# One encoder kernel on one core: a third tap group on TensorE, its taps one step later, the bias table moved to POOL's and SP's queues, and a projection of two products per weight tile in place of three

## The chip, the cores and the metric

The kernel runs on one core of one Trainium2 chip. The time is that of one execution on the device, in microseconds (us). The kernel before took 2296.82 us, the median of three runs (2295.39 to 2298.47). PE is TensorE (PEld its weight loads), DVE is VectorE, ACT is ScalarE, POOL is GpSimd and SP is SyncE. SP computes nothing here; it issues DMAs. A name with a q behind it (ACTq, SPq) is that engine's queue of instructions, in which DMA issues stand.

## The reference

Input x is 256 tokens of 2048 channels, float32. There are two layers, each a mixer and a feed-forward part, with RMS norms in front and residual sums behind:

```python
for i in range(2):
    h = rmsnorm(x, mix_norm[i])
    m = conformer_conv(h, ...) if i == 0 else diff_attention(h, ...)
    x = x + m
    h = rmsnorm(x, ffn_norm[i])
    x = x + conv_ffn(h, ...)        # 2048 -> 2 x 5632, 3 causal taps, silu(gate) * val, -> 2048
return rmsnorm(x, final_norm_g)

def conformer_conv(h):              # the mixer of layer 0
    a, gate = split(h @ w_in + b_in)            # 2048 -> 2 x 2048
    u = causal_dwconv(a * sigmoid(gate), dw_w)  # 31 taps for each channel
    return silu(layernorm(u)) @ w_out + b_out

def diff_attention(h):              # the mixer of layer 1: 16 heads, two 64-wide maps each
    # scores + bias[head, bucket(k - q)], masked by chunks of 64,
    # softmax(first) - lambda * softmax(second), times v, rmsnorm, @ w_o
```

## The kernel before, in words

Activations lie transposed: channels on the 128 partitions, 256 tokens along the free axis. Every large product is made of float32 values split into a high and a low part (`hi`, `lo` for weights, index 0 and 1 of an activation tile for x), and is the sum hi*x_hi + hi*x_lo + lo*x_hi.

Weights come in steps of 512 KB (four 128-row blocks of 256 columns). For each step, SP loads `raw` (5 buffers, `load_w`), ACT copies it into `hi` (6 buffers), and DVE or POOL subtracts to get `lo` (6 buffers, `split_w`, lines 142 to 154). The loop `run` goes through the steps; before the products of step s it has the weights of step s+4 prepared. Four steps make one output tile pair (`pair`), accumulated in a PSUM tile `pp` (2 buffers). After the products of a step, work that was put down with `at(n, ...)` n steps earlier is issued, then six depthwise taps on DVE (`tap_step`), then, at the last step of a pair, its `post`.

In `pair` there are two ways to make the products of one weight block. With `merged` there are three products of 256 columns, all into the same 256 columns of PSUM (line 217). Without it, `hi` is multiplied by x_hi and x_lo side by side, 512 columns (lines 224 and 226), and `lo` by x_hi into the second 256 columns (lines 223 and 227); the two halves of PSUM are added afterwards. The projection w_in of layer 0's mixer is `merged`.

That projection has 16 tiles of four steps. `post` of tile i takes it out of PSUM times the norm's factor (line 436, DVE), makes the sigmoid (line 438, ACT), and writes u into `cpad[i % 3]` (line 440, DVE). Then the depthwise convolution of 31 taps starts. The first 4*G[i] taps are made on PE: u is stored to DRAM (`ud`, line 452), read back four times with shifts (`R`, line 456; both DMAs are issued by ACT), and multiplied by small diagonal matrices `dg`, which POOL makes (line 458). `taps` (line 470) does these products, `at(4)` after `post`. The remaining 31 - 4*G[i] taps are additions on DVE (line 513). The list G was 2 for tiles 0 to 10, then 3, 3, 5, 6, and 0 for the last tile, which goes another way (`last_taps`). Behind the last tile stand a layer norm and the product with w_out.

`attn_setup` (line 719) is called ahead of the first step of layer 0's feed-forward part. It loads a one-hot table and the relative bias, multiplies them, and stores the result 128 times into a DRAM table `d1` of 3 MB (line 732; in the trace the table is called d and its source Z). Much later, in the attention, `bias(h)` reads a skewed 128x256 block of it for each head (`bm`, line 809) and POOL sets one corner to the mask value (line 810). All of these DMAs are issued by ACT. The norm ahead of the feed-forward part gets its factor from a power on POOL (`rsqrt_cols`, line 286), and ACT copies it into `rstd` (line 348).

The order on each engine is made by a list scheduler that simulates the program; it moved the first two `bm` reads far ahead of the attention. Within `with tc.high_priority()` instructions are preferred.

Of the kernel before, what the change touches and what calls it, by code (L numbers as in the profile page):

```python
# [8 lines left out]
F32 = mybir.dt.float32  # L9
F32R = mybir.dt.float32r  # L10
AF = mybir.ActivationFunctionType
ALU = mybir.AluOpType
AX = mybir.AxisListType
ET = mybir.EngineType
P = 128
S = 256
# [5 lines left out]
MASK = -1.0e30  # L22
# [3 lines left out]
class Cfg:  # L26


    def __init__(self, d, f, kc=4):
        self.D, self.F = d, f  # L30
        self.KT = d // P
        self.FT = f // P
        self.H = d // (2 * HD)
        self.KC = kc
        self.NW = kc * 256
        self.kcs = [(i, kc) for i in range(0, self.KT, kc)]
        full = self.KT // 2
        first = self.FT % full or full
        self.chunks = [(0, first)] + [(i, full) for i in range(first, self.FT, full)]
        self.VK = kc // 2  # L40
        self.NA, self.NB = self.KT + self.KT // 2 + 1, 8

        self.G = [2] * (self.KT - 5) + [3, 3, 5, 6, 0]

        self.ND = 18

# [15 lines left out]
class Builder:  # L62
# [363 lines left out]
    def conv_module(self, nin, nout):  # L426
        c, a = self.c, self.a
        nc = self.nc
        KT = c.KT
# [2 lines left out]

        def post(i, ps):
            with self.tc.high_priority():
                t = self.b2("E")
                nc.vector.tensor_tensor(t, ps[:, :, 0:S], nin["rstd"].unsqueeze(1).to_broadcast([P, 2, S]), ALU.mult)
                sg = self.b1("G")
                nc.scalar.activation(sg, t[:, 1, :], AF.Sigmoid, bias=self.col("bin", KT + i))
                u = self.cpad[i % 3]
                nc.vector.scalar_tensor_tensor(u[:, CK - 1:CK - 1 + S], t[:, 0, :], self.col("bin", i), sg, ALU.add,  # L440
                                               ALU.mult)
                if i == KT - 1:
                    nc.scalar.activation(self.c2(), sg[:, 0:2], AF.Silu)
            gm = max(c.G)
            if i == KT - 1:
                self.at(0, lambda: last_taps(u, dgl))
                return

            g = c.G[i]
            n = 4 * (g - 1) + S  # L450
            ud = self.dr.tile([P, UW], F32, tag="ud", name=self.nm("ud"), bufs=2)
            nc.scalar.dma_start(ud, u)
            R = self.ph1.tile([P, 4, 4 * (gm - 1) + S], F32, tag="R", name=self.nm("R"), bufs=2)
            udv = ud.rearrange("(j c) n -> c j n", j=4)
            for s in range(4):
                nc.scalar.dma_start(R[s * 32:(s + 1) * 32, :, :n], udv[:, :, s:s + n])  # L456
            dg = self.ph1.tile([P, 4 * gm, 32], F32, tag="dg", name=self.nm("dg"))[:, :4 * g, :]
            nc.gpsimd.tensor_tensor(dg, self.cmask.unsqueeze(1).to_broadcast([P, 4 * g, 32]),
                                    self.col("wq", 4 * sum(c.G[:i]), 4 * g).unsqueeze(2).to_broadcast([P, 4 * g, 32]), ALU.mult)
            self.at(4, lambda: taps(i, u, R, dg))  # L460
            if i == 0:

                for j in range(0, c.ND, 4):
                    t = self.b2("Y" if j < 16 else "A").rearrange("p a (b s) -> p (a b) s", b=2)[:, :min(4, c.ND - j), :]
                    n = t.shape[1]
                    nc.gpsimd.tensor_tensor(t, self.ident.unsqueeze(1).to_broadcast([P, n, P]),
                                            self.col("cw", (KT - 1) * CK + j, n).unsqueeze(2).to_broadcast([P, n, P]), ALU.mult)
                    dgl.extend(t[:, x, :] for x in range(n))
# [174 lines left out]
        off = 0  # L643
        for i in range(KT):
            off = self.pair(a["w_in"], off, c.kcs, lambda k: nin["xh"][k], lambda ps, i=i: post(i, ps),
                            lo="v" if i == 0 else "vg" if i == 1 else "g", merged=True)
        off = 0
        for pr in range(KT // 2):
            def post2(ps, pr=pr):
                self.x_add(ps, pr, bias="bout")  # L650
                self.x_done(nout, pr)
                if pr == KT // 2 - 1:
# [3 lines left out]
                            lo="g" if pr < 2 else "v")  # L656
# [62 lines left out]
    def attn_setup(self):  # L719

        nc, c, a = self.nc, self.c, self.a
        H = c.H
        rb = self.ph2.tile([NB, H], F32, name="rb")
        nc.scalar.dma_start(rb, a["relb"])
        oh = self.b2("Z").rearrange("p a s -> p (a s)")[:NB, :384]
        nc.scalar.dma_start(oh, a["oneh"])
        ps = self.psx("o", [P, 384])
        nc.tensor.matmul(ps[:H, :], rb, oh, start=True, stop=True)
        tb = self.b2("Z").rearrange("p a s -> p (a s)")[:H, :384]
        nc.vector.tensor_copy(tb, ps[:H, :])  # L730
        d1 = self.dr.tile([H, P, 384], F32, name="d1")
        nc.scalar.dma_start(d1, tb.unsqueeze(1).to_broadcast([H, P, 384]))
        self.bflat = d1.rearrange("h p d -> (h p d)")
        lm = self.c2()
        nc.vector.tensor_tensor(lm[:HD], self.col("lam", 0, 2)[:HD], self.col("lam", 2, 2)[:HD], ALU.mult)
        ps = self.psx("o", [P, 2])
        nc.tensor.matmul(ps, self.ones[:HD, :], lm[:HD], start=True, stop=True)
        e = self.c2()
        nc.scalar.activation(e, ps, AF.Exp)
        self.nlam = self.const.tile([P, 1], F32, name="nlam")  # L740
        nc.vector.tensor_tensor(self.nlam, e[:, 1:2], e[:, 0:1], ALU.subtract)
        nc.vector.tensor_scalar(self.nlam, self.nlam, -LAMBDA_INIT, None, ALU.add)
        self.sg = self.const.tile([P, 1], F32, name="subg")
        nc.vector.tensor_scalar(self.sg, self.col("subg", 0), 1.0 - LAMBDA_INIT, None, ALU.mult)
        self.AT = []
        for i in range(2):
            self.AT.append((self.ph2.tile([P, 2, S], F32R, name=f"at{i}"), self.ph2.tile([P, P], F32, name=f"au{i}")))

    def attention(self, nin, nout):
        c, a = self.c, self.a  # L750
        nc = self.nc
        H, KT = c.H, c.KT
        V, U, O = {}, {}, {}

        def v_group(g, off):
            box = {}
# [47 lines left out]
            self.at(2, lambda: scores(h, q, k, qk))  # L804

        def bias(h):
            bm = self.ph2.tile([P, S], F32, tag="bm", name=self.nm("bm"), bufs=2)
            o = h * P * 384 + P - 1
            nc.scalar.dma_start(bm, self.bflat[o:o + P * 383].rearrange("(p d) -> p d", d=383)[:, :S])
            nc.gpsimd.memset(bm[0:64, S - 64:], MASK)  # L810
            return bm

        def scores(h, q, k, qk):
            bm = bias(h)
            ps = [self.psx("s", [P, 2, S]) for _ in range(2)]

            comp = [slice(cc * HD, (cc + 1) * HD) for cc in range(2)]
# [63 lines left out]
        off = voff = 0  # L881
        for h in range(H):
            if h % 4 == 0:
                voff = v_group(h // 4, voff)
            off = self.pair(a["w_qk"], off, c.kcs, lambda k: nin["xh"][k], lambda ps, h=h: qk_post(h, ps))
        off = 0
        held = []
        for pr in range(KT // 2):
# [146 lines left out]
```

## Time and profile before

| | |
|---|---|
| median of three runs | 2296.82 us |
| the profiled execution's own time | 2303.02 us |
| its span (first to last instruction) | 2300.4 us |
| PE busy | 2224.6 us, 97% |
| DVE, ACT, POOL busy | 73%, 52%, 12% |
| mean granted TensorE clock | 0.985 of full speed |
| DMA | 417.15 MB, 181 GB/s |

Busy time is the union of an engine's instructions. Where one engine fills the span, only its idle stretches and the time of its own instructions can shorten the run. The projection w_in with its taps lies between 6 and 262 us, the layer norm ends at 286 us, the product with w_out at about 381 us. The first feed-forward part begins there, and the attention lies in the stretch from about 1130 to 1490 us.

### The profile page before, as it was taken

The numbers are of one execution on the slowest core, as the hardware profiler recorded it, in microseconds if no ns is written. First come the engines' busy times: TensorE is split into PE (matmuls) and PEld (weight loads), VectorE is DVE, ScalarE is ACT, GpSimd is POOL, SyncE is SP. The second block draws the span as 40 slices with busy tenths as digits, with TensorE's granted clock in tenths as the row PEclk, the third lists the DMA queues.
The fourth block names the chain that finished last, engine by engine and source line by source line (L and its number), as shares of the span: only waits on it lengthen the run. The fifth ranks groups of instructions, "written<-read, shape, count | busy, mean of one in ns | idle before, by whom it ended". The sixth has DMA issues, their size and how long they took to land.

```text
span 2300.4 us, 34637 instructions
## 1 busy us (share of the span) xinstructions
PE 2224.6 (97%) x13294; PEld 1947.9 (85%) x13294; DVE 1670.9 (73%) x2539; ACT 1205.7 (52%) x1788; POOL 281.4 (12%) x189
## 2 busy tenths in 40 slices
PE   6899799799999999999999999999999999999998
PEld 6788688688888888888888888888888888888887
DVE  5788876577777767677766777677777777676774
ACT  5333265455555555455655555555555555554554
POOL 5678510000000000000111011010000000000002
PEclk9999899899999999999999999999999999999999
DMA  6766356766666666666655555466666666666663
GB/s 230 195 193 190 111 159 179 191 198 187 190 188 188 187 188 190 188 190 188 188 179 159 168 168 166 140 200 183 189 188 190 186 190 185 191 187 190 189 187 100
DMA packets 126885, 417.15 MB, mean 181 GB/s; under 512 B 14176, under 2 KB 28288, under 8 KB 126720
## 3 DMA queue, kind: packets, MB, share of 16 engines
q1 hardware_dynamic: 110736, 398.30, 56.8%
q10 hardware_dynamic: 15984, 16.65, 3.5%
q8 instruction: 104, 1.70, 0.3%
q14 instruction: 61, 0.50, 0.1%
HBM read 407.44 MB, written 7.45 MB: 180 GB/s over the span
## 4 chain that ended last, share of the span: by engine, by line
PE 88%; DMA 5%; DVE 4%; issue 1%; ACTq 0%; ACT 0%; POOL 0%; POOLq 0%; SPq 0%; DVEq 0%
PE pp L226 47%; PE pp L227 24%; PE pp L224 4%; PE pp L217 3%; PE pp L223 2%; DMA R<-ud 2%; DMA ud<-cpad 2%; DMA d<-Z 2%; PE pp L774 1%; PE pp L775 1%; PE pp L776 1%; DVE s L513 1%; DVE cpad L440 1%; PE s L475 0%; ACTq L456 0%
## 5 line engine op out<-in xcount | busy, mean ns | idle before, releaser
L226 PE MATMUL pp<-act,hi 128*128 128x512 f32 x3902 | 1382.9, 396 | 21.1 <-DVE E L256 13.0
L227 PE MATMUL pp<-act,lo 128*128 128x256 f32 x3902 | 1096.5, 281 | 0.0
L150 ACT CAST hi<-raw 128x1024 fp32r<-128x1024 f32 x752 | 787.6, 1049 | 536.0 <-PE pp L226 179.3
L152 DVE TENSOR_TENSOR lo<-raw,hi 128x1024 fp32r<-128x1024 f32 x686 | 844.3, 1231 | 283.0 <-ACT hi L150 281.2
L226 PEld LDWEIGHTS pp<-act,hi 128*128 128x128 f32 x3902 | 733.3, 188 | 182.9 <-DVE E L256 13.3
L227 PEld LDWEIGHTS pp<-act,lo 128*128 128x128 f32 x3902 | 739.1, 189 | 10.4
L226 PE MATMUL pp<-actb,hi 128*128 128x512 f32 x856 | 306.7, 396 | 0.0
L227 PE MATMUL pp<-actb,lo 128*128 128x256 f32 x856 | 240.4, 281 | 0.0
L321 POOL TENSOR_TENSOR ssq<-ssq,Z 128x512 f32<-128x512 f32 x24 | 35.6, 1481 | 1532.1 <-ACT Z L317 1532.0
L217 PE MATMUL pp<-act,hi 128*128 128x256 f32 x1088 | 209.3, 294 | 11.4 <-ACT act L267 6.0
L217 PEld LDWEIGHTS pp<-act,hi 128*128 128x128 f32 x1088 | 178.0, 200 | 19.3 <-DVE act L268 6.6
L226 PEld LDWEIGHTS pp<-actb,hi 128*128 128x128 f32 x856 | 160.6, 188 | 38.3 <-issue 0.6
L152 POOL TENSOR_TENSOR lo<-raw,hi 128x1024 fp32r<-128x1024 f32 x66 | 159.4, 2434 | 56.0 <-ACT hi L150 52.4
L256 DVE TENSOR_TENSOR E<-pp,E 128x512 f32<-128x512 f32 x104 | 71.8, 690 | 128.2 <-ACT E L254 127.9
L227 PEld LDWEIGHTS pp<-actb,lo 128*128 128x128 f32 x856 | 161.5, 189 | 0.2
L217 PE MATMUL pp<-act,lo 128*128 128x256 f32 x544 | 158.4, 291 | 2.8 <-DVE lo L152 2.8
L254 ACT COPY E<-pp 128x512 f32<-128x512 f32 x104 | 60.8, 585 | 186.9 <-PE pp L224 161.6
L370 ACT COPY E<-pp 128x512 f32<-128x512 f32 x109 | 63.9, 586 | 169.5 <-PE pp L224 161.8
L677 DVE SCALAR_TENSOR_TENSOR Y<-fpad,prm,Y 128x256 f32<-128x256 f32 x352 | 146.7, 477 | 0.0
L372 DVE TENSOR_TENSOR x<-pp,x 128x512 f32<-128x512 f32 x101 | 69.7, 690 | 89.4 <-ACT E L370 89.0
L674 ACT ACTIVATE Y<-fpad,prm 128x256 f32<-128x256 f32 x176 | 96.3, 596 | 48.2 <-DVE fpad L670 48.2
L513 DVE SCALAR_TENSOR_TENSOR s<-cpad,cprm,s 128x256 f32<-128x256 f32 x214 | 97.5, 482 | 24.8 <-PE s L475 22.6
(218 smaller groups left out, 1890.8 us busy)
## 6 DMA issues: line engine op xcount, KB each, us to landing
raw<-in_w_up_dram SPq DMA_DIRECT2D x352, 512.0 KB, 4.0
raw<-in_w_down_dram SPq DMA_DIRECT2D x176, 512.0 KB, 4.0
raw<-in_w_in_dram SPq DMA_DIRECT2D x64, 512.0 KB, 4.5
raw<-in_w_qk_dram SPq DMA_DIRECT2D x64, 512.0 KB, 3.6
raw<-in_w_out_dram SPq DMA_DIRECT2D x32, 512.0 KB, 4.1
raw<-in_w_v_dram SPq DMA_DIRECT2D x32, 512.0 KB, 3.7
raw<-in_w_o_dram SPq DMA_DIRECT2D x32, 512.0 KB, 3.7
R<-ud ACTq DMA_DIRECT2D x44, 130.0 KB, 5.1
```

Of the source, the lines that this page charges most:

```text
L150: nc.scalar.copy(hi[:, :n], raw[:, :n])
L152: eng.tensor_tensor(lo[:, :n], raw[:, :n], hi[:, :n].bitcast(F32), ALU.subtract)
L217: nc.tensor.matmul(ps[:, 0:S], w[:, kk, cs], xt[:, x, :], start=(k == first and n == 0), stop=(k == last and n == 2))
L224: nc.tensor.matmul(*main, start=False, stop=True)
L226: nc.tensor.matmul(*main, start=(k == first), stop=False)
L227: nc.tensor.matmul(*corr, start=False, stop=False)
L256: nc.vector.tensor_tensor(t, ps[:, :, 0:S], cs, ALU.add)
L370: nc.scalar.copy(cs, ps[:, :, S:])
L372: nc.vector.tensor_tensor(x, ps[:, :, 0:S], x, ALU.add)
L513: nc.vector.scalar_tensor_tensor(acc, u[:, j:j + S], self.col("cw", i * CK + j), acc, ALU.mult, ALU.add)
L674: nc.scalar.activation(y[:, j, :], u[:, j, FK - 1:], AF.Identity, scale=self.col("fw", ch * FK + FK - 1), bias=self.col("fb", ch))
L677: nc.vector.scalar_tensor_tensor(y[:, j, :], u[:, j, q:q + S], self.col("fw", ch * FK + q), y[:, j, :], ALU.mult, ALU.add)
```

## The change

- G is 3 for tiles 0 to 12: eleven tiles get one more group of taps on PE and four fewer on DVE.
- The projection w_in is made with one product of 512 and one of 256 columns per weight block, but for the last tile. `post` now copies the second half of PSUM out (ACT), adds it to the first half in PSUM, and multiplies there too; sigmoid and u read from PSUM.
- `taps` of tiles 0 to 13 are issued five steps after `post` in place of four.
- `attn_setup` issues its three DMAs from POOL in place of ACT, and writes the mask value into the table itself, with 16 further DMAs from POOL.
- `bias(h)` reads its block through SP, ahead of the first step of head h, in place of ACT and just ahead of the scores; the memset on POOL goes.

```diff
-        self.G = [2] * (self.KT - 5) + [3, 3, 5, 6, 0]
+        self.G = [3] * (self.KT - 3) + [5, 6, 0]
...
         def post(i, ps):
             with self.tc.high_priority():
-                t = self.b2("E")
-                nc.vector.tensor_tensor(t, ps[:, :, 0:S], nin["rstd"].unsqueeze(1).to_broadcast([P, 2, S]), ALU.mult)
+
+                t = ps[:, :, 0:S]
+                if i < KT - 1:
+                    cs = self.b2("E")
+                    nc.scalar.copy(cs, ps[:, :, S:])
+                    nc.vector.tensor_tensor(t, t, cs, ALU.add)
+                nc.vector.tensor_tensor(t, t, nin["rstd"].unsqueeze(1).to_broadcast([P, 2, S]), ALU.mult)
...
-            self.at(4, lambda: taps(i, u, R, dg))
+            self.at(5 if i < KT - 2 else 4, lambda: taps(i, u, R, dg))
...
-                            lo="v" if i == 0 else "vg" if i == 1 else "g", merged=True)
+                            lo="v" if i == 0 else "vg" if i == 1 else "g", merged=i == KT - 1)
...
-        nc.scalar.dma_start(rb, a["relb"])
+        nc.gpsimd.dma_start(rb, a["relb"])
         oh = self.b2("Z").rearrange("p a s -> p (a s)")[:NB, :384]
-        nc.scalar.dma_start(oh, a["oneh"])
+        nc.gpsimd.dma_start(oh, a["oneh"])
...
-        nc.scalar.dma_start(d1, tb.unsqueeze(1).to_broadcast([H, P, 384]))
+        nc.gpsimd.dma_start(d1, tb.unsqueeze(1).to_broadcast([H, P, 384]))
         self.bflat = d1.rearrange("h p d -> (h p d)")
+
+        mk = self.ph2.tile([64, 64], F32, name="mk")
+        nc.gpsimd.memset(mk, MASK)
+        for h in range(H):
+            o = h * P * 384 + P - 1
+            nc.gpsimd.dma_start(self.bflat[o:o + 64 * 383].rearrange("(p d) -> p d", d=383)[:, S - 64:S], mk)
...
         def bias(h):
-            bm = self.ph2.tile([P, S], F32, tag="bm", name=self.nm("bm"), bufs=2)
+            BM[h] = self.ph2.tile([P, S], F32, tag="bm", name=self.nm("bm"), bufs=2)
             o = h * P * 384 + P - 1
-            nc.scalar.dma_start(bm, self.bflat[o:o + P * 383].rearrange("(p d) -> p d", d=383)[:, :S])
-            nc.gpsimd.memset(bm[0:64, S - 64:], MASK)
-            return bm
+            d = nc.sync.dma_start(BM[h], self.bflat[o:o + P * 383].rearrange("(p d) -> p d", d=383)[:, :S])
+            self.tc.keep_in_program_order(d)

         def scores(h, q, k, qk):
-            bm = bias(h)
+            bm = BM.pop(h)
...
-            off = self.pair(a["w_qk"], off, c.kcs, lambda k: nin["xh"][k], lambda ps, h=h: qk_post(h, ps))
+            off = self.pair(a["w_qk"], off, c.kcs, lambda k: nin["xh"][k], lambda ps, h=h: qk_post(h, ps),
+                            pre=lambda h=h: bias(h))
```

## Rows read from the trace of the kernel before

**Rows 1.** The page, part 1: busy time of each engine.

```profile
PE 2224.6 (97%) x13294; PEld 1947.9 (85%) x13294; DVE 1670.9 (73%) x2539; ACT 1205.7 (52%) x1788; POOL 281.4 (12%) x189
```

**Rows 2.** Windows: start and end, length, busy time of each engine, clock, DMA.

```profile
66.30:239.50 173.20, 157.33 (x1362) 147.70 (x1360) 147.28 (x318) 59.12 (x69) 134.78 (x72) 0.98 0.68 190
...
400.00:450.00 50.00, 36.99 (x207) 32.21 (x206) 23.31 (x37) 19.01 (x29) 0.99 (x3) 0.86 0.77 174
500.00:600.00 100.00, 100.00 (x574) 87.53 (x573) 77.20 (x108) 56.71 (x79) 0.00 (x0) 1.00 0.62 187
1200.00:1450.00 250.00, 250.00 (x1436) 210.67 (x1435) 184.79 (x396) 142.35 (x304) 25.73 (x37) 1.00 0.55 165
```

**Rows 3.** What PE waited for from 66.3 to 239.5 us: total, times, longest.

```profile
PE s L475 <- DMA R<-ud: 6.2, 5, 2.3
PE t L475 <- DMA R<-ud: 6.0, 3, 2.6
PE s L475 <- issue: 3.2, 1, 3.2
```

**Rows 4.** The chain that ended last, 125 to 139.5 us: start, length, piece.

```profile
125.73 0.69 DVE E L436
...
127.64 1.16 DVE cpad L440
...
128.83 2.40 DMA ud<-cpad
...
132.56 6.06 DMA R<-ud
```

**Rows 5.** The same chain, 195 to 216 us.

```profile
195.81 0.59 DVE E L436
...
198.63 1.10 PE s L475 x16
...
200.63 0.54 DVE cpad L440
201.20 5.07 DMA ud<-cpad
...
207.67 5.00 DMA R<-ud
...
212.80 1.50 PE t L475 x24
```

**Rows 6.** Groups by line and shape, 66.3 to 239.5 us: busy, mean ns, idle before.

```profile
L152 POOL TENSOR_TENSOR lo<-raw,hi 128x1024 fp32r<-128x1024 f32 x48 | 114.9, 2409 | 39.5 <-ACT hi L150 35.9 <-DMA raw<-in_w_in_dram 3.6
...
L440 DVE SCALAR_TENSOR_TENSOR cpad<-E,prm,G 128x256 f32<-128x256 f32 x12 | 17.7, 1474 | 0.0
```

**Rows 7.** The page, part 5: sum of the PSUM halves elsewhere.

```profile
L256 DVE TENSOR_TENSOR E<-pp,E 128x512 f32<-128x512 f32 x104 | 71.8, 690 | 128.2 <-ACT E L254 127.9
...
L254 ACT COPY E<-pp 128x512 f32<-128x512 f32 x104 | 60.8, 585 | 186.9 <-PE pp L224 161.6
```

**Rows 8.** Timeline of ACT, 376 to 450 us.

```profile
391.33 0.67 ACTq L732 DMA_DIRECT2D d<-Z  x1
...
401.69 1.05 ACT L150 CAST hi<-raw 128x1024 fp32r<-128x1024 f32 x1 [2.21 <-PE pp L226]
426.94 0.84 ACTq L809 DMA_DIRECT2D bm<-d  x2
427.82 0.59 ACT L254 COPY E<-pp 128x512 f32<-128x512 f32 x1 [25.08 <-DMA d<-Z]
```

**Rows 9.** Timeline of POOL in the same stretch.

```profile
400.90 0.70 POOL L286 TENSOR_TENSOR rc<-c,mhalf 128x2 f32<-128x2 f32 x1 [25.41 <-DVE c L285]
```

**Rows 10.** DMA queues, 398 to 402 us: packets, MB, share of 16 engines.

```profile
q10 hardware_dynamic: 250, 0.38, 91.3%
```

**Rows 11.** DMA queues, 412 to 418 us; q1 carries SP's loads.

```profile
q1 hardware_dynamic: 336, 1.22, 49.9%
```

**Rows 12.** DMA issues of the whole run: count, KB each, us to landing.

```profile
d<-Z ACTq DMA_DIRECT2D x1, 3072.0 KB, 35.6
```

More of the change, by code (lines that the diff above doesn't have):

```diff
@@ L752, in attention @@
         H, KT = c.H, c.KT
-        V, U, O = {}, {}, {}
+        V, U, O, BM = {}, {}, {}, {}
         def v_group(g, off):
```

## The prediction, made before the changed kernel was run

> **What bounds the kernel now.** I read the page first: TensorE (PE) is busy 97% of the span [rows 1], so only stretches in which PE idles or runs slowly, and the time of its own products, can give anything. The windows find these stretches [rows 2]. In the attention PE is busy for all of 250 us, and a plain stretch of the feed-forward part passes 574 products in 100 us: nothing that is moved off another engine there can pay. Two stretches are loose. From 66.3 to 239.5 us (tiles 3 to 14 of the projection w_in with their taps) PE is busy 157.3 of 173.2 us. And from 400 to 450 us it passes 207 products where 287 belong.
>
> The waits say what the first loses: PE stood 15.4 us in front of the tap products, nearly all for R, the shifted copy that comes back from DRAM [rows 3]. The chain shows why R is late [rows 4]: from the projection's eviction (125.73) through u, the store and the load it takes until 138.62, about one tile. In another tile there is a knot besides [rows 5]: the eviction at 195.81 is prompt, but u is only written at 200.63, since DVE has additions in front of it that need the previous tile's taps, and those run on PE at 198.63, when their own R has come. One late R delays the next.
>
> The second stretch is one event [rows 8]. ACT issues the table's store at 391.33. The scheduler has put the attention's first two bm reads on ACT soon behind it, and the store takes 35.6 us to land [rows 12]. ACT stands 25.08 us, its next copy out of PSUM comes at 427.82, and PE runs dry for want of a PSUM buffer.
>
> **The projection, part by part.** Fewer products: at the feed-forward part's rate an unmerged tile is 64 products at 0.174 us, 11.15 us [rows 2]. A third tap group: 24 products in 1.50 us in place of 16 in 1.10 [rows 5], 0.4 us more of PE for each of the eleven tiles. From 66.3 to 239.5 us PE then needs 12 x 11.15 = 133.8 us, and for taps, 288 products in place of 208 (the 1362 there less 12 x 96 and two others, plus ten groups of eight) at 0.0625 us, 18.0 us: 151.8 us. The whole margin is 173.2 - 151.8 = 21.4 us, almost all of it idle time and not work.
>
> How much idle stays depends on R. With taps five steps after post, PE has five steps and the taps of the tile before to do meanwhile: 5/4 x 11.15 + 1.5 = 15.4 us. The knot is gone as well, because post of the next tile now stands ahead of the taps in the program. Against it stands the way of u: copy 0.59 and add 0.69 are new [rows 7], then multiplication 0.69, sigmoid and u about 1 us together, some 1.3 us of queues and handoffs, the store 2.4 to 5.1, four issues 1.5, the load 5.0 to 6.1 [rows 4, 5]: between 13 and 17.5 us, in the middle some 15.7. Since a wait for one R also gives the next more time, the loss for each tile is half of the excess, so 0 to 1.1 us. I take 0.5, or 6 us for twelve tiles. Gain 21.4 - 6 = 15.4, rounded 15; bounds 5 (every DMA slow, and ACT late with the copy) and 21 (no wait left).
>
> Is another engine in the way at the new pace, 158 us for the twelve tiles? POOL works 134.8 us there [rows 2], mostly lo at 2.41 us each [rows 6]; larger dg tiles add under 2 us. That is 87%, close, but POOL prepares four steps ahead, and PE never waited for it there. DVE has 147.3 us; it loses ten times four additions of 0.4 us (16) and gains twelve adds (8): 139 us. The write of u could fall too: 1.47 us now with two inputs from SBUF [rows 6], while the eviction from PSUM beside it takes 0.69 [rows 4]. PSUM is held about 2 us longer for each tile, which the other buffer covers for 11 us.
>
> On this write the Trainium skill has a rule (SBUF — State Buffer, Who interferes with whom): a DVE instruction with at most one SBUF input does not contend with GpSimd. This trace agrees so far as it goes, 0.69 us with PSUM and 1.47 without; by the rule u would take about 0.5 us, 1 us less in the way of R, and by the rows alone anything between 0.5 and 1.5.
>
> Startup and tail I put at nothing, within 3 us. At the end post of the last tile waits on DVE behind statistics of the tile before, which the change leaves; taps of tile 13 come a step later there, but PE waited about as long for them.
>
> **The table.** Without bm reads on ACT the 25 us stand is gone. PE lost 80 products of 287 in that window: 80 x 0.174 = 13.9 us [rows 2]. I take all of it. One thing could keep a part: while the table is stored, its queue holds 91% of the DMA engines and SP's weight loads move nothing [rows 10], later the two share and the weights get 1.22 MB in 6 us [rows 11], 203 GB/s, enough for the 187 that the feed-forward part moves [rows 2]. PE's last prepared step was cast at 401.69 [rows 8], and PE ran on to about 416 from what was prepared; the loads that came then would just do. If the starving repeats worse, some 5 us come back.
>
> On this, the Trainium skill (DMA: Bandwidth & Descriptors, Queues, rings and completion order) says that each DMA engine goes round between the queues it has work for. The later rows agree, near half and half; the earlier ones, with one queue alone at 91%, do not. By the rule nothing of the 13.9 us would come back; by the earlier rows up to 5.
>
> POOL is nearly empty in the feed-forward part (0.99 us busy of 50 [rows 2]), and hides the 16 mask writes as long as its power for the norm at 400.90 [rows 9] does not come behind them.
>
> **bm by SP.** A bm read on SP waits until the scores two heads earlier are done, and the weight loads queue behind it. SP runs about five steps ahead, 5 x 2.79 = 13.9 us, and a load lands in about 4. So some 10 us of wait are covered; I expect 2 to 5, hence nothing. Without that cover each microsecond would stop PE, sixteen times. The issues and memsets taken from ACT and POOL in the attention are worth nothing beside a full PE.
>
> **Sum.** 15 + 14 = 29 us. The profiled execution took 2303.0 us, so 2274 for it; it lay 6.2 us above the median of the runs, and against 2296.8 the same sum gives 2268.
>
> **The rivals.**
>
> *POOL's power behind the mask writes.* `attn_setup` stands in the program ahead of the norm's power. Every mask write must wait for the table to land. If POOL's queue holds them in front, the power comes at 391.3 + 35.6 plus sixteen issues at some 0.5 us, near 435, or near 470 if the store shares the DMA engines and takes twice as long. ACT waits for the factor with the weight copies behind it, and PE stops from about 419: 17 to 53 us in place of 13.9. The far end costs 39 us more than now against the 15 gained: 2297 + 24 = 2321. It decides from about 448 on, where the loss eats the 15. For it: the power comes only 9.6 us after the store's issue, and the scheduler once already believed the store to be done by then. Against: it believed so after the power, not before, as the reads stood behind a cast of 401.69.
>
> *POOL held by the store itself.* No DMA of this trace is issued by POOL, so the price of issuing 3 MB there is open: at least the 0.67 us of ACT's issue [rows 8], at most the 35.6 us of the transfer [rows 12]. The first is nearer, since ACT's queue went on to other work at once. At the far end the power comes at about 428, PE stops some 10 us, and of the 14 us only 4 are gained: 2278.
>
> The Trainium skill speaks against the move here (DMA: Bandwidth & Descriptors, SWDGE vs HWDGE vs iDMA): the descriptors of a GpSimd DMA are written by software on that engine, those of the other two by hardware. No run here shows it yet; it is the mechanism by which this rival would come.
>
> *Taps still wait.* If R comes later by as much as the taps do, for instance because ACT, which issues both DMAs and now the copy, is late, the change doesn't do what it is for: gain 4 in the projection, 14 at the table, 2279.
>
> **Chances.** Forecast 0.53; POOL held 0.20; taps still wait 0.12; power behind the mask writes 0.13; anything else 0.02. The forecast's own range is 2258 to 2277, and with the second and third 2256 to 2288. A measurement of this kernel can tell about 0.2%, 4.6 us. The first three are all faster; of the fourth a quarter may end near no change. So faster 0.85, same 0.04, slower 0.11.
>
> **What would show it.** In the projection: PE's waits for R under 7 us in place of 15, tiles 13.2 us apart in place of 14.4, u written in about 0.5 us. At the table: no wait of ACT for d, 280 products or more in the 50 us after it, POOL's power within 12 us of the store's issue. In the attention: PE full, SP's waits at bm short. The prediction is wrong if PE idles over 10 us at the start of the first feed-forward part, or if the twelve tiles take over 165 us.

## The result, and the profile after

The changed kernel takes 2271.21 us (median of four runs, 2267.83 to 2273.51) and the kernel before, on the same chip, 2297.64 (2295.39 to 2298.93): ratio 0.9885, 95% interval 0.9867 to 0.9902. It is faster, and the time lies 3 us from the forecast of 2268, within both of its ranges (2258 to 2277, and 2256 to 2288). The profiled execution took 2273.51 us against 2303.02, its span is 2271.7 against 2300.4: 28.7 us less. The question is whether these came from where the prediction had them.

The page's part 1, which answers to [rows 1]: PE still fills the span.

```profile
PE 2216.7 (98%) x12902; PEld 1917.1 (84%) x12902; DVE 1654.0 (73%) x2510; ACT 1212.1 (53%) x1803; POOL 292.2 (13%) x193
```

The windows that answer to [rows 2]. A tile's eviction, used here as a mark of time, is the start of its multiplication by the norm's factor (line 436 before, 441 now). The first window runs from the eviction of tile 3 to that of tile 14, the second and third lie in the first feed-forward part, the others are the plain feed-forward stretch and the attention. The numbers are those of [rows 2]: start and end, length, busy time of PE, PEld, DVE, ACT and POOL, granted clock, DMA share and GB/s.

```profile
80.60:225.20 144.60, 141.44 (x977) 115.84 (x977) 123.18 (x259) 59.12 (x74) 124.80 (x66) 1.00 0.74 209
...
380.00:430.00 50.00, 45.75 (x255) 39.48 (x254) 31.28 (x48) 24.61 (x37) 9.15 (x17) 0.97 0.92 208
...
410.00:415.00 5.00, 2.40 (x9) 1.87 (x8) 4.67 (x8) 3.75 (x8) 4.25 (x9) 0.73 0.95 359
500.00:600.00 100.00, 100.00 (x574) 87.59 (x573) 77.18 (x109) 56.83 (x79) 0.00 (x0) 1.00 0.59 189
1200.00:1450.00 250.00, 250.00 (x1461) 212.74 (x1460) 180.45 (x379) 140.72 (x297) 25.51 (x25) 1.00 0.53 163
```

In the projection PE is busy for 141.44 of 144.60 us. In the kernel before the same eleven tiles took 159.70 us (79.8 to 239.5), with PE busy for 144.61: 15.1 us gained, of which 11.9 were idle time (15.1 before, 3.2 now) and 3.2 PE's busy time. The kernel before there:

```profile
79.80:239.50 159.70, 144.61 (x1250) 135.97 (x1250) 133.85 (x290) 54.25 (x64) 127.27 (x68) 0.98 0.69 191
```

At the start of the feed-forward part a loss is left: 255 products in 50 us where 287 belong, and PE at work for 2.40 us of the five after 410. The plain stretch and the attention are as before.

The prediction's stretch was one tile longer: twelve tiles, from the eviction of tile 2 at 66.3 us. Over these the changed kernel takes 164.7 us in place of 173.2, and gains 8.5 us only:

```profile
66.29 0.69 DVE L436 TENSOR_TENSOR E<-pp,rstd 128x512 f32<-128x512 f32 x1 [1.90 <-PE pp L217]
```

```profile
60.45 0.69 DVE L441 TENSOR_TENSOR pp<-pp,rstd 128x512 f32<-128x512 f32 x1
```

```profile
60.50:225.20 164.70, 155.68 (x1063) 126.88 (x1062) 135.40 (x288) 64.26 (x80) 136.78 (x73) 0.98 0.73 206
```

One stall of the start has changed its side. In the kernel before PE waits 4.9 us for R at 58.8 us, ahead of the eviction of tile 2; in the changed one that eviction comes 5.8 us earlier, and PE waits 5.9 us for R at 67.1, behind it. At the eviction of tile 3 the two kernels are level again, 0.8 us apart, so the comparisons below begin there.

PE's waits in the projection, 80 to 225 us, which answer to [rows 3]: 3.0 us where 15.1 stood over the same eleven tiles.

```profile
PE t L480 <- issue: 1.6, 1, 1.6
PE s L480 <- DMA R<-ud: 1.4, 2, 1.3
```

Over the prediction's twelve tiles, with the 5.9 us at 67.1, they are 8.9 us where 15.4 stood.

The chain of one tile whose R comes late, beside [rows 4, 5], and the groups of the tile's work, beside [rows 6, 7]:

```profile
174.81 0.47 ACT G L443
175.31 0.50 DVE cpad L445
175.83 4.66 DMA ud<-cpad
...
181.88 5.90 DMA R<-ud
...
187.92 1.50 PE s L480 x24
```

```profile
L445 DVE SCALAR_TENSOR_TENSOR cpad<-pp,prm,G 128x256 f32<-128x256 f32 x12 | 5.8, 483 | 3.7 <-ACT G L443 3.4 <-DMA raw<-in_w_in_dram 0.3
...
L440 DVE TENSOR_TENSOR pp<-pp,E 128x512 f32<-128x512 f32 x12 | 8.4, 699 | 11.6 <-ACT E L439 11.6
...
L439 ACT COPY E<-pp 128x512 f32<-128x512 f32 x12 | 7.0, 585 | 8.7 <-PE pp L224 8.7
```

The knot of [rows 5] is gone: u is written 0.03 us after the sigmoid. The two DMAs are no faster, 4.66 and 5.90 us; PE simply comes to the taps later.

ACT at the start of the feed-forward part, which answers to [rows 8]: the first eviction, the waits that are left, and the next evictions.

```profile
373.14 0.59 ACT L254 COPY E<-pp 128x512 f32<-128x512 f32 x1 [2.77 <-PE pp L224]
...
398.56 1.05 ACT L150 CAST hi<-raw 128x1024 fp32r<-128x1024 f32 x1 [11.43 <-DMA raw<-in_w_up_dram]
...
405.05 1.04 ACT L150 CAST hi<-raw 128x1024 fp32r<-128x1024 f32 x1 [3.46 <-DMA raw<-in_w_up_dram]
...
410.47 0.58 ACT L254 COPY E<-pp 128x512 f32<-128x512 f32 x1
```

No wait for d stands there any more. ACT now waits for weights, 11.43 us in one piece. POOL's timeline, which answers to [rows 9]:

```profile
372.38 1.03 POOL L737 DMA_DIRECT2D d<-Z  x1 [15.28 <-DVE Z L735]
381.64 0.71 POOL L286 TENSOR_TENSOR rc<-c,mhalf 128x2 f32<-128x2 f32 x1 [8.23 <-DVE c L285]
409.01 4.25 POOL L744 DMA_DIRECT2D d<-mk  x8 [26.66 <-DMA d<-Z]
414.01 4.19 POOL L744 DMA_DIRECT2D d<-mk  x8 [0.74 <-DMA d<-mk]
```

The store's issue holds POOL for 1.03 us, the power comes 9.3 us after the issue began, and the mask writes stand behind it. The DMA queues from 378 to 390 and from 390 to 402 us (packets, MB, share; q0 is POOL's store, q1 SP's weight loads), beside [rows 10, 11], and the issues beside [rows 12]:

```profile
q0 software_dynamic: 255, 1.18, 98.7%
raw<-in_w_up_dram SPq DMA_DIRECT2D x3, 512.0 KB, 26.8
```

```profile
q0 software_dynamic: 238, 1.10, 81.2%
q1 hardware_dynamic: 234, 0.89, 18.1%
...
d<-Z POOLq DMA_DIRECT2D x1, 3072.0 KB, 36.3
```

For 12 us the weights get nothing, for the next 12 they get 0.89 MB. That is where PE's loss after 400 us comes from; it begins at 405 us, ahead of the first mask write at 409.01.

From the evictions of the two traces the 28.7 us are made up thus (us). A feed-forward eviction is the copy of line 254, by ACT.

| stretch | before | after | gained | predicted |
|---|---|---|---|---|
| start to eviction of tile 3 | 79.83 | 80.59 | -0.8 | 0 |
| tile 3 to tile 14 | 159.7 | 144.6 | 15.1 | 15 |
| tile 14 to tile 15 | 22.6 | 16.2 | 6.3 | 0 |
| tile 15 to first feed-forward eviction | 130.3 | 131.7 | -1.4 | 0 |
| first to ninth feed-forward eviction | 105.6 | 97.1 | 8.5 | 14 |
| the rest | | | 1.0 | 0 |

The 15 us were predicted from tile 2 on. With the boundary there the first two rows gain 5.8 and 8.5.

### The profile page after: what moved, and what is told of

It is laid out like the page before. It is cut to its first block, busy times and chain, and to the rows that moved or that the text cites. A ratio compares the mean times of both kernels' runs of the same rounds, so it can differ in the third digit from the quotient of the medians.

```text
span 2271.7 us, 33836 instructions
## 1 busy us (share of the span) xinstructions
PE 2216.7 (98%) x12902; PEld 1917.1 (84%) x12902; DVE 1654.0 (73%) x2510; ACT 1212.1 (53%) x1803; POOL 292.2 (13%) x193
## 4 chain that ended last, share of the span: by engine, by line
PE 91%; DMA 5%; POOL 1%; DVE 1%; issue 1%; ACT 0%; ACTq 0%; SPq 0%; POOLq 0%; DVEq 0%
PE pp L226 50%; PE pp L227 26%; PE pp L224 4%; PE pp L223 2%; DMA R<-ud 2%; PE pp L785 1%; PE pp L787 1%; PE pp L786 1%; DMA raw<-in_w_up_dram 1%; DMA ud<-cpad 1%; POOL lo L152 1%; PE pp L217 1%; PE t L480 0%; PE s L480 0%; DMA raw<-in_w_in_dram 0%
## 5 line engine op out<-in xcount | busy, mean ns | idle before, releaser
L226 PE MATMUL pp<-act,hi 128*128 128x512 f32 x4352 | 1547.3, 397 | 22.4 <-DVE act L268 9.4
L227 PE MATMUL pp<-act,lo 128*128 128x256 f32 x4352 | 1225.9, 282 | 1.7 <-DVE lo L152 1.7
L226 PEld LDWEIGHTS pp<-act,hi 128*128 128x128 f32 x4352 | 820.5, 189 | 209.2 <-DVE act L268 10.6
L227 PEld LDWEIGHTS pp<-act,lo 128*128 128x128 f32 x4352 | 828.1, 190 | 12.9 <-DVE lo L152 2.0
L226 PE MATMUL pp<-actb,hi 128*128 128x512 f32 x856 | 306.9, 396 | 0.9 <-ACT hi L150 0.9
L682 DVE SCALAR_TENSOR_TENSOR Y<-fpad,prm,Y 128x256 f32<-128x256 f32 x352 | 146.8, 477 | 0.0
L518 DVE SCALAR_TENSOR_TENSOR s<-cpad,cprm,s 128x256 f32<-128x256 f32 x182 | 86.4, 486 | 19.6 <-PE s L480 15.6
L224 PE MATMUL pp<-act,hi 128*128 128x512 f32 x248 | 92.5, 397 | 0.1
L224 PE MATMUL pp<-actb,hi 128*128 128x512 f32 x208 | 77.4, 395 | 0.0
L377 DVE TENSOR_TENSOR x<-x,E 128x512 f32<-128x512 f32 x109 | 75.1, 689 | 2.8
```

What stands on the lines that cost most here:

```text
L224: nc.tensor.matmul(*main, start=False, stop=True)
L226: nc.tensor.matmul(*main, start=(k == first), stop=False)
L227: nc.tensor.matmul(*corr, start=False, stop=False)
L377: nc.vector.tensor_tensor(x, x, cs, ALU.add)
L518: nc.vector.scalar_tensor_tensor(acc, u[:, j:j + S], self.col("cw", i * CK + j), acc, ALU.mult, ALU.add)
L682: nc.vector.scalar_tensor_tensor(y[:, j, :], u[:, j, q:q + S], self.col("fw", ch * FK + q), y[:, j, :], ALU.mult, ALU.add)
```

## The experiments

Twelve kernels take the edits apart, each timed against the kernel before on the same chip. "Tiles" is the time from tile 3 to tile 14, "table" that from the first to the ninth feed-forward eviction, both from the profiled execution. Undisturbed, "table" is 89.3 us (eight tiles, as q4 has them).

| run | us | before | ratio, 95% | tiles | table |
|---|---|---|---|---|---|
| p1_projection_only | 2285.52 | 2298.92 | 0.9945 (0.9926 to 0.9963) | 148.8 | 106.9 |
| p2_table_only | 2290.24 | 2298.92 | 0.9956 (0.9943 to 0.9968) | 158.3 | 96.5 |
| p3_taps_at_four | 2282.85 | 2298.92 | 0.9927 (0.9907 to 0.9946) | 155.0 | 95.8 |
| p4_three_products | 2275.03 | 2298.92 | 0.9891 (0.9873 to 0.9910) | 146.8 | 96.4 |
| q1_taps_later_alone | 2277.04 | 2302.81 | 0.9895 (0.9879 to 0.9912) | 141.3 | 106.8 |
| q2_two_groups | 2268.93 | 2302.81 | 0.9858 (0.9841 to 0.9876) | 143.7 | 95.7 |
| q3_store_by_act | 2268.65 | 2302.81 | 0.9857 (0.9841 to 0.9872) | 148.2 | 90.8 |
| q4_table_early | 2266.48 | 2302.81 | 0.9844 (0.9829 to 0.9860) | 146.9 | 89.3 |
| r1_power_behind_masks | 2282.61 | 2301.95 | 0.9915 (0.9902 to 0.9928) | 144.6 | 105.4 |
| r2_step_and_sp | 2260.83 | 2301.95 | 0.9824 (0.9808 to 0.9840) | 143.0 | 90.8 |
| r3_two_products_store_act | 2261.51 | 2301.95 | 0.9828 (0.9811 to 0.9845) | 140.0 | 90.8 |
| r4_changed_again | 2272.17 | 2301.95 | 0.9871 (0.9857 to 0.9885) | 142.4 | 97.2 |

**The two halves of the change.** p1 makes the projection's four edits alone on the kernel before: these three and the new `post`. p2 is the changed kernel with the same four undone.

```diff
-        self.G = [2] * (self.KT - 5) + [3, 3, 5, 6, 0]
+        self.G = [3] * (self.KT - 3) + [5, 6, 0]
...
-            self.at(4, lambda: taps(i, u, R, dg))
+            self.at(5 if i < KT - 2 else 4, lambda: taps(i, u, R, dg))
...
-                            lo="v" if i == 0 else "vg" if i == 1 else "g", merged=True)
+                            lo="v" if i == 0 else "vg" if i == 1 else "g", merged=i == KT - 1)
```

> The kernel before with the projection's edits alone (G, two products, taps a step later); the table as before. From the two traces the projection up to the first feed-forward part is 19.3 us shorter, of it 15 in the tiles and 6 at the tail, less 2 at the start and in the norm. If that is the projection's own doing, this kernel takes 2297.6 - 19 = 2278 us, and the 25 us stand of ACT at the table stays. If the tail's 6 us came from the table's move, as POOL's order shifted, it takes about 2284.

> The changed kernel with the projection as before: the table's edits alone. By the two traces the table is worth 8.5 us: 2289. By the prediction's term it is worth 13.9: 2284. If the two parts of the change overlap (a stall hidden by the other), it is nearer 2293.

Each half is worth something alone, 13.4 and 8.7 us by the medians. The product of the ratios is 0.9901, the whole change 0.9885 and in r4 0.9871: the whole gives 0.2 to 0.3% more than the two halves, which is about what the intervals leave open. p1 came out near its second figure, 2284, but not for the reason given there: its tail, 15.9 us from tile 14 to 15, is as short as in the changed kernel, and what it lacks is lost from tile 3 to 14 (148.8 us in place of 144.6) and up to the feed-forward part (133.9 in place of 131.7). In p1 ACT stands at the table as before,

```profile
ACT E L254 <- DMA d<-Z: 25.2, 1, 25.2
```

and in p2 "table" falls to 96.5 us: the 25 us stand belongs to the table's half and to nothing else.

**Which edit of the projection.** Four kernels. p3 is the changed kernel with the taps at the old step:

```diff
-            self.at(5 if i < KT - 2 else 4, lambda: taps(i, u, R, dg))
+            self.at(4, lambda: taps(i, u, R, dg))
```

> The changed kernel with the taps four steps after post again. If the later taps are what frees the tiles, PE's waits for R from tile 3 to 14 come back to 12 to 20 us and the time is 2271 + 10 to 14, about 2283. If the two products or the third group did it, and the step is of no account, it stays within 3 us of 2271.

p4 is the changed kernel with three products in every tile, and with the old `post`:

```diff
-                            lo="v" if i == 0 else "vg" if i == 1 else "g", merged=i == KT - 1)
+                            lo="v" if i == 0 else "vg" if i == 1 else "g", merged=True)
```

> The changed kernel with the projection merged again (three products of 256 columns, eviction to SBUF as before). If the form of the products matters only by PE's own time, a tile takes 11.5 in place of 11.15 us, 15 tiles 5 us: 2276. If the write of u matters besides (two SBUF inputs, 1.47 in place of 0.48 us, later R), R waits grow and it is 2280 or more. If the shorter way of the merged form (no copy, no add) outweighs both, it is 2271 or less.

q1 is the kernel before with the later step and nothing else:

```diff
-            self.at(4, lambda: taps(i, u, R, dg))
+            self.at(5 if i < KT - 2 else 4, lambda: taps(i, u, R, dg))
```

> The kernel before with one edit: taps five steps after post. If the step is what breaks the knot, whatever the form of the products, this alone gives most of the projection's gain: 2298 - 9 to 12, about 2288. If it needs the smaller DVE load of the third group, it gives 4 or less: 2294 or more. The taken-away step cost 11.6 us in the changed kernel.

q2 is the changed kernel with the old list of tap groups:

```diff
-        self.G = [3] * (self.KT - 3) + [5, 6, 0]
+        self.G = [2] * (self.KT - 5) + [3, 3, 5, 6, 0]
```

> The changed kernel with two tap groups on PE in tiles 0 to 10 again. PE saves 11 x 0.43 = 4.7 us of products, DVE gets 44 additions of 0.4 to 0.5 us more, 18 to 22 us. If PE sets the pace once taps are late, it is no slower than 2271 and may come to 2267. If the chain of DVE additions (23 in a row at 0.5 us, 11.5 us of a 13 us tile, besides the eviction) sets it, it is 2276 or more.

The step alone does it. Without it, p3, PE's waits for R come back in part and tiles 3 to 14 take 10 us longer than in the changed kernel. These are its longest waits, 80 to 225 us; over its own eleven tiles, which end at 235.8, those for R are 8.4 us, less than the 12 to 20 expected:

```profile
PE t L480 <- DMA R<-ud: 3.8, 2, 2.7
PE s L480 <- DMA R<-ud: 3.5, 2, 2.0
PE t L480 <- DVE pp L441: 2.6, 1, 2.6
```

With it alone, q1, one wait of 0.8 us is left, PE is busy for 140.52 of 141.30 us from tile 3 to 14, and the kernel gains 25.8 us, more than twice the 9 to 12 expected and nearly twice what all four edits of the projection gain in p1. The two were timed on different chips, and 3.9 of the 12.4 us between the two gains lie in the times of the kernel before (2302.81 and 2298.92). In the traces p1 is 7.7 us longer, and 7.5 of that lie in tiles 3 to 14, where PE waits 4.0 us for one R ahead of tile 14; but its next tile is 3.9 us shorter than q1's, so that up to tile 15 it is 3.6 us behind:

```profile
PE s L475 <- DMA R<-ud: 0.8, 1, 0.8
```

```profile
79.20:220.50 141.30, 140.52 (x1248) 132.35 (x1247) 129.18 (x287) 53.39 (x64) 126.51 (x67) 1.00 0.79 217
```

The other two edits act on PE's busy time in those eleven tiles, in opposite senses. With two groups it is 140.52 us with three products (q1) and 137.85 with two (q2); with three groups and two products, as in the change, 141.44. So two products save about 2.7 us, and the third group costs 3.6 back. r2 and r3, both with two groups, repeat the first: 140.64 us with three products, 137.57 with two. q2 and p3 over their own eleven tiles:

```profile
81.12:224.82 143.70, 137.85 (x903) 113.22 (x902) 126.66 (x303) 59.50 (x74) 123.93 (x67) 1.00 0.77 211
```

```profile
80.86:235.83 154.97, 144.03 (x966) 117.07 (x958) 124.06 (x261) 60.21 (x74) 126.37 (x67) 0.98 0.72 195
```

In the total, two products are not to be seen: p4 stands at 0.9891 beside the change's 0.9885. The third group tends to cost: 0.9858 without it (q2), 0.9871 and 0.9885 with it, though the intervals overlap.

**The table.** q3 is the changed kernel with table and store back on ACT's queue; bm stays on SP, and POOL masks each block, so no mask write goes to DRAM:

```diff
-        nc.gpsimd.dma_start(d1, tb.unsqueeze(1).to_broadcast([H, P, 384]))
+        nc.scalar.dma_start(d1, tb.unsqueeze(1).to_broadcast([H, P, 384]))
...
             self.tc.keep_in_program_order(d)
+            nc.gpsimd.memset(BM[h][0:64, S - 64:], MASK)
```

> The changed kernel with the table's loads and store issued by ACT again, and the mask set by POOL in each block; only the bm reads stay on SP. If the gain at the table is only that the two early bm reads are off ACT's queue, the time stays within 3 us of 2271, and the weight loads wait 17 us or more behind the store as they do with POOL's. If POOL's queue is what helps, ACT or SP stands again at the store and it is 2276 or more.

q4 is the changed kernel with the table made and stored, still by POOL, behind the last tile of the projection (`table()`, called in `last_taps`, holds what `attn_setup` did), and with the mask writes issued eight steps later and behind the norm's power. The product for the table now uses one of the `pp` tiles, and ACT in place of DVE copies it out (not shown in this cut):

```diff
+            self.table()
...
+                with self.tc.issue_after(self.last_pow.ins):
+                    nc.gpsimd.dma_start(self.bflat[o:o + 64 * 383].rearrange("(p d) -> p d", d=383)[:, S - 64:S], mk)
```

> The changed kernel with the table made behind the last tile of the projection, at about 245 us, where the DMA engines are 15% busy, and the mask writes held behind the power of the feed-forward norm. If the 5.4 us that the prediction's 13.9 fell short by are the store starving the weight loads, it is 2271 - 5 = 2266, PE loses under 1 us at the start of the feed-forward part, and no weight load takes 20 us there. If the store starves the loads of the w_out product as much, it stays at 2271. If the loss has another cause, PE still loses 4 to 6 us where it does now.

q3 was expected within 3 us of the change; its ratio, 0.9857, is better than the 0.9885 and 0.9871 of the change. In q3 "table" is 90.8 us, 1.5 above undisturbed. These are the 50 us in which the changed kernel passed 255 products, and the queues from 378 to 390 and 390 to 402 us (q10 is now the store):

```profile
380.00:430.00 50.00, 50.00 (x291) 43.89 (x290) 38.05 (x58) 30.44 (x44) 0.70 (x1) 1.00 0.93 243
```

```profile
q10 hardware_dynamic: 758, 1.16, 92.7%
raw<-in_w_up_dram SPq DMA_DIRECT2D x3, 512.0 KB, 17.5
...
q10 hardware_dynamic: 669, 1.03, 53.7%
q1 hardware_dynamic: 620, 2.28, 46.7%
```

The store lands after 36.3 us in both kernels. But in the second 12 us the weights get 2.28 MB beside ACT's store and 0.89 beside POOL's. So the gain at the table comes from the bm reads leaving ACT's queue; moving the store to POOL's queue took about 6 us of it back (97.1 against 90.8). The other traces agree: with the store on POOL's queue and nothing else done to it "table" is 95.7 to 97.2 us (six kernels), with the store on ACT's and the reads on SP's it is 90.8 (q3, r2, r3). r2 and q1 differ in the reads alone: 90.8 and 106.8. Two things stay together in all of them: the reads went to SP, and they keep their place in the program's order. Whether reads on ACT's queue that stay in order would do as well wasn't tried.

q4 shows the same from the other side: with the store out of the way nothing is lost in the feed-forward part.

```profile
365.00:415.00 50.00, 50.00 (x292) 43.95 (x291) 36.37 (x52) 26.71 (x38) 9.17 (x18) 1.00 0.63 191
```

The sixteen mask writes lie in this stretch too, from 381.4 us, and PE loses nothing beside them; so they are hardly what the changed kernel loses. The first feed-forward eviction of q4 comes 135.8 us after tile 15 in place of 131.7, so some 4 of the 8 us are lost again around the layer norm, where its table is made; that stretch wasn't taken apart. Nor is the total a measure of the table alone: from the ninth feed-forward eviction to the end q4 takes 1796.1 us, the changed kernel 1801.4 and all others 1801 to 1803, although no edit of q4 was meant for that part. From 1550 to 2200 us its PE passes 3740 products and the changed kernel's 3717, both without idle time. The cause of these 5 us is open.

**The rival of the mask writes, made to happen.** r1 is the changed kernel with POOL's power held behind the sixteenth mask write:

```diff
+        with self.tc.issue_after(mk.ins):
             self.nc.gpsimd.tensor_tensor(dst, v, self.mhalf, ALU.pow)
```

> The changed kernel with one order forced: POOL's power for the feed-forward norm behind the 16 mask writes. This is the prediction's slower rival, made to happen. The store lands 36 us after its issue and the 16 writes take POOL 8.5 us more, so the power comes some 46 us after the store's issue in place of 9; ACT waits for the factor with the weight copies behind it. PE would stop about 19 us in place of the 8 that the changed kernel loses now: 2271 + 11, about 2282. If a late power costs nothing, it stays at 2271.

```profile
405.83 4.23 POOL L750 DMA_DIRECT2D d<-mk  x8 [35.60 <-DMA d<-Z]
410.77 4.23 POOL L750 DMA_DIRECT2D d<-mk  x8 [0.71 <-DMA d<-mk]
415.01 0.72 POOL L292 TENSOR_TENSOR rc<-c,mhalf 128x2 f32<-128x2 f32 x1
```

```profile
PE o L280 <- POOL rc L292: 8.5, 1, 8.5
```

The power comes at 415.0, "table" is 105.4 as in the kernel before, and the run loses 10.4 us against the changed kernel on the same chip (r4). The mechanism of the rival is real and its price over the changed kernel is 8 us at the table (105.4 against 97.2) and 10 in the total: it would have eaten the table's gain, and not made the kernel slower than before.

**What is best.** r2 puts the two parts that were shown to pay on the kernel before: the later step, and bm by SP with the store left on ACT. r3 is r2 with the change's two products per weight block and its `post`, r4 is the changed kernel once more. r2's diff:

```diff
-            self.at(4, lambda: taps(i, u, R, dg))
+            self.at(5 if i < KT - 2 else 4, lambda: taps(i, u, R, dg))
...
-            nc.scalar.dma_start(bm, self.bflat[o:o + P * 383].rearrange("(p d) -> p d", d=383)[:, :S])
-            nc.gpsimd.memset(bm[0:64, S - 64:], MASK)
-            return bm
+            d = nc.sync.dma_start(BM[h], self.bflat[o:o + P * 383].rearrange("(p d) -> p d", d=383)[:, :S])
+            self.tc.keep_in_program_order(d)
+            nc.gpsimd.memset(BM[h][0:64, S - 64:], MASK)
...
+                            pre=lambda h=h: bias(h))
```

> The kernel before with two edits alone: taps a step later, and bm read by SP ahead of its head; store by ACT, three products, two tap groups. If these two carry the whole gain, and the other edits give nothing or cost, it is the fastest of all: 2298 - 24 (the step alone) - 15 (the table's whole loss of 16 less 1.5) = about 2259. If the two products and the third group are needed beside a freed table, it is 2266 or more.

> As the kernel with the step and SP alone, with the projection's two products per weight block added (two tap groups). If the product form is worth PE's own 0.35 us for each of 15 tiles, it is 4 to 5 us faster than that one. If the copy and add that it needs, and the weights' faster use, give that back, the two are within 3 us.

> The changed kernel unaltered, on the chip of these runs, as the mark for the other three: 0.9885 of the kernel before, about 2271, within its interval.

r2 is the fastest kernel, 2260.83 us, 0.9824 of the kernel before (0.9808 to 0.9840), 11.3 us under the changed kernel on the same chip; the intervals don't meet. At the table its PE is never idle:

```profile
365.00:415.00 50.00, 50.00 (x290) 43.72 (x289) 34.99 (x54) 29.69 (x42) 0.70 (x1) 1.00 0.93 227
```

r3 ties with it. r3 and q3 differ in the list of tap groups alone: 0.9828 against 0.9857, the same direction as q2, again with intervals that overlap a little (0.9845, 0.9841). Two pairs with one sign make a cost of the third group likely, 3 to 7 us; neither alone shows it. The traces go the same way: with the later step, tiles 3 to 14 take 140.0 to 143.7 us with two groups (four kernels) and 142.4 to 148.8 with three (seven).

## Why the prediction came out

**Projection: the size right from tile 3 on, the reason half right.** Predicted were 15 us for the twelve tiles from the eviction of tile 2, in 158 us. These took 164.7, just inside the 165 that was named as a sign of being wrong, and gained 8.5: PE was busy for 155.7 us of them in place of 151.8, and idle for 9.0 in place of 6. Most of what is missing is the wait of 5.9 us that moved in from the start. From tile 3 to 14, where the two kernels can be compared, 15.1 us were gained and the tiles are 13.15 us apart (13.2 predicted). The waits for R, 1.4 us there, fell under 7 us as predicted; over the twelve tiles they are 7.3. (In the rows before, R was behind 12.2 of the 15.4 us, the other 3.2 were "issue"; "nearly all" says too much.)

The step "taps five steps after post" carries all of it (q1, p3). "Fewer products" and "a third tap group" were costed as work of PE, 157.3 to 151.8 us for twelve tiles; from tile 3 to 14, PE's busy time went from 144.61 to 141.44, and q1, with neither edit, has 140.52. p3, which has both edits and waits again, has 144.03. So that fall came from the stalls being gone, and the two edits cancel within 1 us. The granted clock goes with it: its mean over these tiles is 0.98 in the kernel before and in p3, 1.00 in q1 and in the change. I had put the three edits into one margin of 21.4 us and not asked what each gives alone; that is why a one-line edit worth the whole gain isn't in the prediction.

**The write of u** takes 0.483 us in place of 1.474 [rows 6], at the low end of the bounds, 0.5 to 1.5. On this the rule of the Trainium skill (SBUF — State Buffer, Who interferes with whom), that a DVE instruction with at most one SBUF input, outside its 2-port modes, doesn't contend with GpSimd, agrees with the trace: POOL was busy for 124.80 of those 144.60 us. What the write is worth in the time isn't shown: p4, with the old write, ties with the change, but p4 also spares the copy and the add, 0.59 and 0.70 us in the way of u.

**Start and tail were missed.** "Startup and tail I put at nothing, within 3 us": up to the eviction of tile 2, where the forecast began, 5.8 us were gained and given back in the next tile (0.8 us lost up to tile 3), and from tile 14 to 15 6.3 us were gained. In the kernel before DVE had four instructions of the layer norm's statistics, from 252.13 to 262.07 us, ahead of the last eviction; in the changed one the eviction stands ahead of the last of them. Before and after:

```profile
259.59 2.56 DVE L568 TENSOR_TENSOR M<-lnsq 128x256 f32<-128x256 f32 x1
262.07 0.68 DVE L436 TENSOR_TENSOR E<-pp,rstd 128x512 f32<-128x512 f32 x1
```

```profile
241.45 0.69 DVE L441 TENSOR_TENSOR pp<-pp,rstd 128x512 f32<-128x512 f32 x1
242.05 1.98 DVE L573 TENSOR_TENSOR M<-lnsq 128x256 f32<-128x256 f32 x1
```

The prediction held that the change leaves this order. The traces say otherwise: the eviction stands ahead of that sum in all eleven kernels with the later step, and behind it in the three without (the kernel before, p2, p3). From tile 14 to 15 the three take 17.7 to 22.6 us and the eleven 15.7 to 19.7. So the new order comes with the step; how much of the 6.3 us it is worth isn't shown, for q1 and r2, with the same projection, differ by 4 us there (19.7 and 15.7). From tile 3 to 15 the step alone takes 161.0 us (q1), the whole change 160.9 and the kernel before 182.2.

**The table is the term that was mis-sized**: 13.9 predicted, 8.5 measured, and 255 products in the 50 us where the prediction wanted 280 or more. PE was idle for 4.3 of these 50 us, under the 10 named as a sign of being wrong. The stand of ACT is gone as said, the power came within 12 us of the store's issue, and the 1.03 us issue on POOL was near the end that I took. What failed is the step "the loads that came then would just do": I gave them the 203 GB/s of [rows 11], measured beside ACT's store, and beside POOL's they had 0.89 MB in 12 us, 74 GB/s (beside ACT's in q3, at the same distance from the store's issue, 190). The 5 us that "come back" if the starving is worse did come back, 5.4. They were named as a risk, for a reason that the rows of before could not show; moving the store's queue, not only the reads, was what made it so (q3).

**bm by SP costs nothing**, as predicted. SP's waits there are 16.4 us in all, the longest 2.6, and PE is full:

```profile
SPq L820 <- DVE smx L842: 9.2, 5, 2.6
SPq L820 <- DVE Z L839: 6.8, 3, 2.3
```

**The rivals.** POOL held by the store: false, 1.03 us. Taps still wait: false, 3.0 us from tile 3 to 14. Power behind the mask writes: did not happen, 381.64 against 409.01; forced, it comes at 415, earlier than the 435 to 470 of the prediction, since the store was issued 22 us earlier (369.20 in place of 391.33); the sixteen issues take 9.2 us together. The 17 to 53 us that I gave were PE's whole loss there; in r1 it is 16 us (105.4 less the undisturbed 89.3), just under the lower end.

The sum, 2274 us for the profiled execution against 2273.5 measured, is better than its terms, and that is luck: 5.4 us too much at the table and 2.2 us of small losses (startup, norm) were made up by 6.3 in the tail and 1.0 in the rest. On the prediction's own boundaries the luck is larger: projection and table gave 8.5 us each where 15 and 14 were forecast, start and tail 5.8 and 6.3 where nothing was.

## What to carry to other kernels

When an engine waits for a round trip through DRAM whose length can't be cut, first ask what it costs to issue the consumer one step later: here that one line alone gained more than it did together with a new product form, a new split of the taps and a faster write (q1 and p1). Cost each edit of a bundle by itself, since two of them may cancel, as the third tap group and the two products did on PE. And when a large store moves to another queue, the question is not only what its issue costs, but what share it leaves to the loads that run beside it.

## What was unexpected of the hardware

The same 3 MB store took 36.3 us from either queue, yet left very different shares to the loads. The packets suggest why: on POOL's queue they are 1.18 MB / 255 = 4.6 KB each, on ACT's 1.16 MB / 758 = 1.5 KB, three times smaller. From 390 to 402 us the two queues alternate nearly one for one, 238 packets to 234 beside POOL, 669 to 620 beside ACT. So the weights get about one packet, 3.7 to 3.8 KB, for each of the store's. By the queues' shares of the engines' time (81.2% for 238 packets, 53.7% for 669) one of the store's packets takes four times as long on POOL's queue as on ACT's, and the weights get 0.89 MB in place of 2.28. The Trainium skill (DMA: Bandwidth & Descriptors, Queues, rings and completion order) says that a DMA engine goes round between its queues packet by packet; these counts agree. The prediction had taken that round for equal shares, whatever the packets' size. That the packet's size, and not something else of POOL's queue, sets the share wasn't tried by itself.

The rule doesn't tell why the loads get nothing at all in the first 12 us beside either store (98.7% and 92.7% of the engines' time, three loads of 512 KB landing after 26.8 and 17.5 us). That stays open.

Kernels with the same code in the projection differ by up to 6 us from tile 3 to 14 (142.4 to 148.8 us for p1, q3, q4, r1, r4 and the changed kernel), so no edit there that is worth less can be settled by one pair of traces. Up to tile 15 they differ by 4 us (160.5 to 164.6).
